# A decoder block with product-key experts: keys of four heads' choices looked up together, and a higher gather pace beside the choices

## The chip, the core and the metric

The kernel runs on one core of a Trainium2 chip. The core has TensorE (PE, matmul; PEld is its weight load), VectorE (DVE), ScalarE (ACT), GpSimd (POOL) and SyncE (SP), each with its own queue that it works off in order, and 16 DMA engines that all queues share. The metric is the device time of one execution in microseconds (us).

## The reference

One layer in float32, 512 tokens by 2048 features. Attention with a decay bias (8 heads) and a matrix-memory cell (4 heads) are projected, normalised and added; then comes the part that this change touches, a retrieval over 128 x 128 single-neuron experts:

```python
q = (xt @ w_q).reshape(T, PEER_HEADS, 2, PEER_KEY_DIM // 2)
scores = jnp.einsum('thpd,pnd->thpn', q, keys)
s_top, i_top = lax.top_k(scores, PEER_TOPK)          # 16 of 128, twice
cand = (s_top[:, :, 0, :, None] + s_top[:, :, 1, None, :])   # 16 x 16 sums
cand_idx = (i_top[:, :, 0, :, None] * PEER_N_KEYS + i_top[:, :, 1, None, :])
s_fin, pos = lax.top_k(cand, PEER_TOPK)              # 16 of the 256 sums
idx = jnp.take_along_axis(cand_idx, pos, axis=-1)    # which experts
gate = jax.nn.softmax(s_fin, axis=-1)
act = gelu(u[idx] . x) * gate;  y = sum(act * v[idx])
```

So for each of 512 tokens and 8 heads two lists of 16 keys are chosen, then 16 pairs out of their 256 sums. A pair's place `pos` is 16 * (place in the first list) + (place in the second); the lookup turns it into two key numbers, and 128 * first + second is the expert.

## The kernel before

The 512 tokens are four tiles of 128. After attention and cell (to about 620 us) comes the output projection, and with it the experts begin. They are worked in two ways at once.

- **Dense, on TensorE.** For token tiles 1 to 3 (less 64 tokens) all 16384 experts are multiplied: 128 blocks of 128 experts. `early_steps` loads a block in two chunks of 512 KB (`raw` or `rawx`, from `uT`); ScalarE rounds each to `hi` (L123), VectorE computes the rest `lo` (L125); 48 matmuls go into `sacc`; ScalarE applies gelu into `es` (L617) and stores 160 KB to `stab`. Later the gate of each chosen pair is spread over a table by one-hot matmuls (`table`, L963 to L973), and the same is done with `v`.
- **Gathered, on VectorE.** For tile 0 and the 64 tokens only the chosen rows are fetched: `gathered` issues one indirect DMA of 128 rows of 2048 floats (1 MB) on GpSimd's queue (L651), up to three rows ahead of their use, into `row` (three buffers) and, from the blocks on, every fourth into `rowx`; then `dot` multiplies it by x and sums (L662).

The two are interleaved by a step counter. `advance(n)` adds n to `state`, and each whole step issues the next gather and the dot product of an earlier row. A block calls it eight times with an eighth of `pace_u`. The paces are constants: 0.4 a hook in the output projection and in w_q, `PACE_EARLY` (1.25) a block beside the choices, 1.6 beside the tables; then what is left of 199 steps is divided over the blocks up to number 114 (26 of them), and the first 64 tokens' tables and `v` follow.

The choices of tiles 1 to 3 stand between. For each head `w_q(h)` multiplies out the queries and the scores of all three tiles; then, tile by tile, 2, 2 and 3 blocks of the dense part are issued (`EARLY_TOPK`) and `choose(t, h, scs)` follows: `top16` twice on 128 scores (five VectorE instructions each), the sum table `cd` on GpSimd (L751), `top16` on 256 sums, and the lookup. The lookup is done twice, for the first and the second list: shift or mask `pos` (L759), cast to float `pf` (L761), subtract 0 to 15 from each on GpSimd into `oh` (L763, 16 x 16), compare with zero and multiply by the list's keys `it` (L766), sum over the list (L769) into `i0f` or `i1f`. At the end `gates` makes a softmax of the scores of each tile, and TensorE transposes `i0f`, `i1f` and `gts` (L952) for the tables. Tile 0 is chosen earlier, between 780 and 960 us, by the same function, and its gathers wait for its heads.

Instructions are issued in the written order but placed on each engine's queue by a scheduler, which orders by readiness in its own model and moves `lo` ahead.

Of the kernel before, what the change touches and what calls it, by code (L numbers as in the profile page):

```python
# [10 lines left out]
F32 = mybir.dt.float32  # L11
# [3 lines left out]
U32 = mybir.dt.uint32  # L15
AF = mybir.ActivationFunctionType
OP = mybir.AluOpType
AX = mybir.AxisListType
PSUM = bass.MemoryType.PSUM

P = 128
S = 512
NT = S // P
# [8 lines left out]
TK = 16  # L32
PH = 8
# [13 lines left out]
EARLY_G = 3  # L47
HOLD = 14
PACE_O = 0.4
PACE_EARLY = 1.25  # L50
PACE_WQ = 0.4
PACE_G = 1.6
PACE_HOLD = 1.0
LAG = 2
LAG_U = 3
AHEAD_LO = 35
U_STEPS = SLOTS + S1 + 2 * LAG_U + 1
NTG = ND // TG

# [31 lines left out]
def block_kernel(ctx: ExitStack, tc: tile.TileContext, a, out):  # L91
    nc = tc.nc
# [7 lines left out]
    iota16 = iota[:, 0:TK]  # L100
# [485 lines left out]
    dots = [pc.tile([P, n], F32, name="dots%d" % t) for t, n in enumerate((SLOTS, S1))]  # L586
    act1 = pc.tile([P, P], F32, name="act1")
    tp = tpool(ctx, "tp")
    i0f = tp.tile([P, NT, PH, TK], F32, name="i0f")
    i1f = tp.tile([P, NT, PH, TK], F32, name="i1f")  # L590
    gts = tp.tile([P, NT, PH, TK], F32, name="gts")
    rows = tpool(ctx, "rows", 3)
    esp = tpool(ctx, "esp", 2)
# [117 lines left out]
    with ExitStack() as rx:  # L711
# [15 lines left out]
                add_block(xq.tile([P, 512], F32, tag="sq5", name="sq5"), acc[j], t, n)  # L727

        n2 = tpool(rx, "n2", 2)
        sc0 = n2.tile([P, PH, 2, P], F32, name="sc0", bufs=1)  # L730

        def top16(vals, idx, src, width):
            s2 = n2.tile([P, width], F32, tag="s2_%d" % width, name="s2")
# [4 lines left out]
            nc.vector.max_index(out=idx[:, 0:8], in_max=vals[:, 0:8], in_values=src)  # L738
            nc.vector.max_index(out=idx[:, 8:16], in_max=vals[:, 8:16], in_values=s2)

        def choose(t, h, scs):

            ii = n2.tile([P, 2, TK], U32, tag="ii", name="ii")
            vt = n2.tile([P, 2, TK], F32, tag="vt", name="vt")
            for j in range(2):
                top16(vt[:, j, :], ii[:, j, :], scs[:, j, :], P)
                yield
            it = n2.tile([P, 2, TK], F32, tag="it", name="it")
            nc.vector.tensor_copy(out=it, in_=ii)
            cd = n2.tile([P, TK, TK], F32, tag="cd", name="cd")  # L750
            nc.gpsimd.tensor_tensor(out=cd, in0=vt[:, 0, :, None].to_broadcast([P, TK, TK]),  # L751
                                    in1=vt[:, 1, None, :].to_broadcast([P, TK, TK]), op=OP.add)
            pos = n2.tile([P, TK], U32, tag="pos", name="pos")
            yield
            top16(gts[:, t, h, :], pos, cd.rearrange("p a b -> p (a b)"), TK * TK)
            yield
            for w, (op, imm) in enumerate(((OP.logical_shift_right, 4), (OP.bitwise_and, 15))):
                pi = n2.tile([P, TK], U32, tag="pi", name="pi")
                nc.vector.tensor_scalar(out=pi, in0=pos, scalar1=imm, scalar2=None, op0=op)  # L759
                pf = n2.tile([P, TK], F32, tag="pf", name="pf")  # L760
                nc.vector.tensor_copy(out=pf, in_=pi)  # L761
                oh = n2.tile([P, TK, TK], F32, tag="oh", name="oh")
                nc.gpsimd.tensor_tensor(out=oh, in0=pf[:, :, None].to_broadcast([P, TK, TK]),  # L763
                                        in1=iota16[:, None, :].to_broadcast([P, TK, TK]),
                                        op=OP.subtract)
                nc.vector.scalar_tensor_tensor(  # L766
                    out=oh, in0=oh, scalar=0.0, in1=it[:, w, None, :].to_broadcast([P, TK, TK]),
                    op0=OP.is_equal, op1=OP.mult)
                nc.vector.tensor_reduce(out=(i0f, i1f)[w][:, t, h, :], in_=oh, axis=AX.X,  # L769
                                        op=OP.add)  # L770
                if w == 1 and t == 0:
                    nc.vector.scalar_tensor_tensor(out=idx0[h], in0=i0f[:, 0, h], scalar=128.0,
                                                   in1=i1f[:, 0, h], op0=OP.mult, op1=OP.add)
                    heads0[0] = h + 1
                yield

        def gates(t):

            g = gts[:, t]
            top = n2.tile([P, PH], F32, tag="top", name="top")  # L780
            nc.vector.tensor_copy(out=top, in_=g[:, :, 0])
            nc.vector.tensor_tensor(out=g, in0=g, in1=top[:, :, None].to_broadcast([P, PH, TK]),
                                    op=OP.subtract)
            nc.scalar.activation(out=g, in_=g, func=AF.Exp)
            gs = n2.tile([P, PH], F32, tag="gs", name="gs")
            nc.vector.tensor_reduce(out=gs, in_=g, axis=AX.X, op=OP.add)
            nc.vector.reciprocal(out=gs, in_=gs)
            nc.vector.tensor_tensor(out=g, in0=g, in1=gs[:, :, None].to_broadcast([P, PH, TK]),
                                    op=OP.mult)
# [70 lines left out]
        def choose0_steps():  # L860
            for h in range(PH):
                while ready[0] <= h:
                    yield
                yield from choose(0, h, sc0[:, h])
            gates(0)

        scores0 = w_q0()
# [53 lines left out]
            next(chosen, None)  # L921
        for _ in chosen:
            pass
        for h in range(PH):
            scs = w_q(h)
            for t in range(1, NT):
                for _ in range(EARLY_TOPK[t - 1]):
                    early_s()
                for _ in choose(t, h, scs[t]):
                    pass  # L930
            if h == PH - 1:
                for t in range(1, NT):
                    gates(t)

        ix = n2.tile([P, SLOTS], I32, name="ix", bufs=1)
        nc.vector.scalar_tensor_tensor(out=ix, in0=flat(i0f[:, 1]), scalar=128.0,
# [255 lines left out]
```

## Time and profile before

| | |
|---|---|
| median of three runs | 3193.15 us (3188.04, 3193.15, 3195.32) |
| the profiled execution | 3191.11 us, its span 3189.3 us |
| granted TensorE clock | 0.992 of full, mean |
| busy: PE, DVE, ACT, POOL | 3108.9, 2324.3, 1274.7, 604.5 us |
| DMA | 835.71 MB, mean 262 GB/s |

The page is read from the totals to the stretches: a busy share over the whole span hides that the stages have different limits. The stages that matter here are the choices of tile 0 (780 to 960 us), those of tiles 1 to 3 with dense blocks (970 to 1500), the tables (1500 to 1790), 26 blocks with many gathers (1790 to 1990, called the full stretch below), and from about 2150 the products with `v`.

### The profile page before, as it was taken

Reading aid. Unit: us, or ns where it says so; the run is one execution under the profiler, and the core shown is the slowest. Engines: PE = TensorE matmul, PEld = TensorE weight load, DVE = VectorE, ACT = ScalarE, POOL = GpSimd, SP = SyncE. Lnnn points to the kernel's source line nnn. Section 1 sums busy time; section 2 is a strip of 40 time slices with the busy share of each in tenths; the row PEclk is TensorE's granted clock in tenths of the full one; section 3 lists DMA queues with packets and bytes.
Section 4 is the critical chain, followed back from the end, with each engine's and each line's share of the span. In section 5 each row is a group of like instructions: output and inputs, shape, how many; then the busy total and the mean of one; then the engine's idle time right before and its main releaser. Section 6 shows DMA issues by size and latency. Waiting matters only on the chain.

```text
span 3189.3 us, 43251 instructions
## 1 busy us (share of the span) xinstructions
PE 3108.9 (97%) x16682; PEld 2737.0 (86%) x16682; DVE 2324.3 (73%) x3251; ACT 1274.7 (40%) x1955; POOL 604.5 (19%) x444
## 2 busy tenths in 40 slices
PE   8999999999989999999999998989999999999998
PEld 6788777787779999999999988978888888888887
DVE  6533333456999999999898988757787777777764
ACT  4432222444443333334888632633333333333332
POOL 0000000100323333333222332112121122222200
PEclk9999999999999999999999999999999999999999
DMA  4222222256878888988999999899888888888753
GB/s 159 75 93 80 79 93 79 74 199 196 306 287 306 314 320 321 325 317 301 335 377 347 398 417 412 294 337 337 299 298 303 317 305 294 297 316 314 267 177 119
DMA packets 246577, 835.71 MB, mean 262 GB/s; under 512 B 21793, under 2 KB 104097, under 8 KB 200737
## 3 DMA queue, kind: packets, MB, share of 16 engines
q1 hardware_dynamic: 178402, 451.24, 41.9%
q0 software_dynamic: 46080, 335.56, 27.2%
q10 hardware_dynamic: 21888, 46.15, 3.8%
q8 instruction: 130, 2.13, 0.3%
q14 instruction: 77, 0.63, 0.1%
HBM read 781.94 MB, written 50.92 MB: 261 GB/s over the span
## 4 chain that ended last, share of the span: by engine, by line
PE 83%; DMA 7%; DVE 6%; issue 2%; ACT 2%; POOL 1%; SPq 0%; DVEq 0%; ACTq 0%; POOLq 0%
PE y L130 24%; PE acc L130 24%; PE sacc L130 20%; PE yk L130 8%; DMA row<-in_u,idx 4%; DVE lo L125 2%; DMA rowx<-in_u,idx 2%; DVE row L662 1%; PE sps L130 1%; PE po L130 1%; DMA sv<-stab 1%; ACT stg L971 1%; DMA gtB<-gtab 1%; ACT hi L123 1%; DMA raw<-in_uT 0%
## 5 line engine op out<-in xcount | busy, mean ns | idle before, releaser
L125 DVE TENSOR_TENSOR lo<-raw,hi 128x1024 fp32r<-128x1024 f32 x649 | 790.6, 1220 | 583.2 <-ACT hi L123 582.7
L123 ACT CAST hi<-raw 128x1024 fp32r<-128x1024 f32 x649 | 681.4, 1050 | 1295.9 <-PE y L130 388.3
L130 PE MATMUL sacc<-x3d,hi 128*128 128x320 f32 x4096 | 926.4, 313 | 4.6 <-ACT hi L123 4.6
L130 PEld LDWEIGHTS sacc<-x3d,hi 128*128 128x128 f32 x4096 | 687.0, 189 | 5.5 <-ACT hi L123 5.4
L130 PE MATMUL sacc<-x3d,lo 128*128 128x320 f32 x2048 | 643.1, 314 | 17.2 <-DVE lo L125 17.0
L130 PEld LDWEIGHTS sacc<-x3d,lo 128*128 128x128 f32 x2048 | 386.4, 189 | 28.9 <-DVE lo L125 28.2
L651 POOL DMA_INDIRECT row<-in_v,idx x128 | 217.4, 1699 | 839.2 <-ACT hi L123 605.2
L130 PE MATMUL y<-hi,wbufA 128*128 128x512 f32 x1152 | 357.7, 391 | 4.7 <-ACT hi L123 4.7
L662 DVE SCALAR_TENSOR_TENSOR row<-row,x 128x2048 f32<-128x2048 f32 x147 | 336.2, 2288 | 20.2 <-DMA row<-in_u,idx 20.1
L130 PE MATMUL y<-hi,wbufB 128*128 128x512 f32 x1128 | 349.1, 389 | 0.0
L692 DVE SCALAR_TENSOR_TENSOR x<-row,dots,x 128x2048 f32<-128x2048 f32 x128 | 300.1, 2344 | 0.0
L651 POOL DMA_INDIRECT row<-in_u,idx x147 | 194.8, 1325 | 500.0 <-ACT hi L123 222.2
L130 PEld LDWEIGHTS y<-hi,wbufA 128*128 128x128 f32 x1152 | 217.4, 189 | 50.5 <-ACT hi L123 5.1
L130 PEld LDWEIGHTS y<-hi,wbufB 128*128 128x128 f32 x1128 | 211.7, 188 | 44.0
L130 PE MATMUL acc<-xT,hi 128*128 128x512 f32 x768 | 244.1, 396 | 0.0
L130 PE MATMUL acc<-hi,xT 128*128 128x512 f32 x768 | 241.9, 393 | 0.0
L130 PE MATMUL y<-lo,wbufA 128*128 128x512 f32 x576 | 225.2, 391 | 1.9 <-DVE lo L125 1.9
L130 PE MATMUL y<-lo,wbufB 128*128 128x512 f32 x564 | 219.4, 389 | 0.0
L170 POOL TENSOR_TENSOR rsr<-rst,mhalf 128x1 f32<-128x1 f32 (+2 forms) x24 | 19.0, 796 | 893.4 <-DVE rst L167 893.4
L130 PEld LDWEIGHTS acc<-hi,xT 128*128 128x128 f32 x768 | 143.8, 188 | 28.7
L130 PEld LDWEIGHTS acc<-xT,hi 128*128 128x128 f32 x768 | 143.9, 189 | 28.4 <-ACT xT L187 0.2
L123 ACT CAST hi<-rawx 128x1024 fp32r<-128x1024 f32 x87 | 91.2, 1051 | 175.3 <-PE sacc L130 102.2
(550 smaller groups left out, 4592.4 us busy)
## 6 DMA issues: line engine op xcount, KB each, us to landing
raw<-in_vS SPq DMA_DIRECT2D x256, 512.0 KB
raw<-in_uT SPq DMA_DIRECT2D x177, 512.0 KB
rawx<-in_uT SPq DMA_DIRECT2D x79, 512.0 KB
raw<-in_w_out SPq DMA_DIRECT2D x64, 512.0 KB
raw<-in_w_q SPq DMA_DIRECT2D x56, 512.0 KB
gtab<-stg ACTq DMA_DIRECT2D x24, 1024.0 KB
stab<-es ACTq DMA_DIRECT2D x128, 160.0 KB
sv<-stab SPq DMA_DIRECT2D x64, 320.0 KB
```

The costliest lines, as they stand in the source:

```text
L123: pace[0] = nc.scalar.copy(out=hi[:, :width], in_=raw[:, :width]).ins
L125: nc.vector.tensor_tensor(out=lo[:, :width], in0=raw[:, :width], in1=hi[:, :width].bitcast(F32), op=OP.subtract)
L130: nc.tensor.matmul(out=o, lhsT=l, rhs=r, start=start, stop=stop)
L170: nc.gpsimd.tensor_tensor(out=r, in0=t, in1=mhalf[:, 0:width], op=OP.pow)
L651: beside(nc.gpsimd.indirect_dma_start(out=row, out_offset=None, in_=a[src], in_offset=bass.IndirectOffsetOnAxis(ap=idx(j), axis=0)))
L662: return nc.vector.scalar_tensor_tensor(out=row, in0=row, scalar=1.0, in1=x30, op0=OP.mult, op1=OP.mult, accum_out=to[:, j:j + 1])
L692: return nc.vector.scalar_tensor_tensor(out=x2[:, 0, :], in0=row, scalar=dots[0][:, j:j + 1], in1=x2[:, 0, :], op0=OP.mult, op1=OP.add)
L971: nc.scalar.copy(out=stg[:, :, q4 * 4:q4 * 4 + 4].rearrange("p i q -> p q i"), in_=gp_)
```

## The change

Three things change.

1. `choose` ends with the third `top16`; its positions go to a buffer (`posb`, four heads by three tiles). The keys of the lists are cast straight into their place in the results, one tile `i01` that holds `i0f` and `i1f`. For tiles 1 to 3 the lookup runs once for four heads: `decode_first` (shift or mask, cast, subtraction on GpSimd, now 128 x 1024) is issued after the fourth head's choice, for both lists; `decode_last` (compare, sum, written over the keys) one interval later, after the next tile's choice. The 128 x 1024 buffers of both lists are the space of `sc0`, the scores of tile 0. Tile 0 keeps a lookup for each head (`choose0`).
2. `pi` and `pf` have one buffer each, not two.
3. `PACE_EARLY` is 1.4, not 1.25. The step counter stands at 106 at the end of the choices where it stood at 98, and what is left for the 26 blocks of the full stretch is 1.73 steps a block where it was 2.04.

```diff
--- before.py
+++ after.py
@@ -47,13 +47,14 @@
 EARLY_G = 3
 HOLD = 14
 PACE_O = 0.4
-PACE_EARLY = 1.25
+PACE_EARLY = 1.4
 PACE_WQ = 0.4
 PACE_G = 1.6
 PACE_HOLD = 1.0
 LAG = 2
 LAG_U = 3
 AHEAD_LO = 35
+HB = PH // 2
 U_STEPS = SLOTS + S1 + 2 * LAG_U + 1
 NTG = ND // TG
 
@@ -586,8 +587,8 @@
     dots = [pc.tile([P, n], F32, name="dots%d" % t) for t, n in enumerate((SLOTS, S1))]
     act1 = pc.tile([P, P], F32, name="act1")
     tp = tpool(ctx, "tp")
-    i0f = tp.tile([P, NT, PH, TK], F32, name="i0f")
-    i1f = tp.tile([P, NT, PH, TK], F32, name="i1f")
+    i01 = tp.tile([P, 2, NT, PH, TK], F32, name="i01")
+    i0f, i1f = i01[:, 0], i01[:, 1]
     gts = tp.tile([P, NT, PH, TK], F32, name="gts")
     rows = tpool(ctx, "rows", 3)
     esp = tpool(ctx, "esp", 2)
@@ -727,7 +728,7 @@
                 add_block(xq.tile([P, 512], F32, tag="sq5", name="sq5"), acc[j], t, n)
 
         n2 = tpool(rx, "n2", 2)
-        sc0 = n2.tile([P, PH, 2, P], F32, name="sc0", bufs=1)
+        sc0 = n2.tile([P, PH, 2, P], F32, tag="sc0", name="sc0", bufs=1)
 
         def top16(vals, idx, src, width):
             s2 = n2.tile([P, width], F32, tag="s2_%d" % width, name="s2")
@@ -738,37 +739,55 @@
             nc.vector.max_index(out=idx[:, 0:8], in_max=vals[:, 0:8], in_values=src)
             nc.vector.max_index(out=idx[:, 8:16], in_max=vals[:, 8:16], in_values=s2)
 
-        def choose(t, h, scs):
+        def choose(t, h, scs, pos):
+
 
             ii = n2.tile([P, 2, TK], U32, tag="ii", name="ii")
             vt = n2.tile([P, 2, TK], F32, tag="vt", name="vt")
             for j in range(2):
                 top16(vt[:, j, :], ii[:, j, :], scs[:, j, :], P)
                 yield
-            it = n2.tile([P, 2, TK], F32, tag="it", name="it")
-            nc.vector.tensor_copy(out=it, in_=ii)
+            nc.vector.tensor_copy(out=i01[:, :, t, h, :], in_=ii)
             cd = n2.tile([P, TK, TK], F32, tag="cd", name="cd")
             nc.gpsimd.tensor_tensor(out=cd, in0=vt[:, 0, :, None].to_broadcast([P, TK, TK]),
                                     in1=vt[:, 1, None, :].to_broadcast([P, TK, TK]), op=OP.add)
-            pos = n2.tile([P, TK], U32, tag="pos", name="pos")
             yield
             top16(gts[:, t, h, :], pos, cd.rearrange("p a b -> p (a b)"), TK * TK)
             yield
-            for w, (op, imm) in enumerate(((OP.logical_shift_right, 4), (OP.bitwise_and, 15))):
-                pi = n2.tile([P, TK], U32, tag="pi", name="pi")
-                nc.vector.tensor_scalar(out=pi, in0=pos, scalar1=imm, scalar2=None, op0=op)
-                pf = n2.tile([P, TK], F32, tag="pf", name="pf")
-                nc.vector.tensor_copy(out=pf, in_=pi)
-                oh = n2.tile([P, TK, TK], F32, tag="oh", name="oh")
-                nc.gpsimd.tensor_tensor(out=oh, in0=pf[:, :, None].to_broadcast([P, TK, TK]),
-                                        in1=iota16[:, None, :].to_broadcast([P, TK, TK]),
-                                        op=OP.subtract)
-                nc.vector.scalar_tensor_tensor(
-                    out=oh, in0=oh, scalar=0.0, in1=it[:, w, None, :].to_broadcast([P, TK, TK]),
-                    op0=OP.is_equal, op1=OP.mult)
-                nc.vector.tensor_reduce(out=(i0f, i1f)[w][:, t, h, :], in_=oh, axis=AX.X,
-                                        op=OP.add)
-                if w == 1 and t == 0:
+
+        def decode_first(w, pos, oh):
+
+            n = pos.shape[1]
+            op, imm = ((OP.logical_shift_right, 4), (OP.bitwise_and, 15))[w]
+            pi = n2.tile([P, HB, TK], U32, tag="pi", name="pi", bufs=1)[:, 0:n]
+            nc.vector.tensor_scalar(out=pi, in0=pos, scalar1=imm, scalar2=None, op0=op)
+            pf = n2.tile([P, HB, TK], F32, tag="pf", name="pf", bufs=1)[:, 0:n]
+            nc.vector.tensor_copy(out=pf, in_=pi)
+            nc.gpsimd.tensor_tensor(
+                out=oh,
+                in0=pf.rearrange("p h k -> p k h")[:, :, :, None].to_broadcast([P, TK, n, TK]),
+                in1=iota16[:, None, None, :].to_broadcast([P, TK, n, TK]), op=OP.subtract)
+
+        def decode_last(w, t, hs, oh):
+
+            keys = i01[:, w, t, hs, :]
+            x = oh.rearrange("p k h i -> p k (h i)")
+            nc.vector.scalar_tensor_tensor(
+                out=x, in0=x, scalar=0.0,
+                in1=keys.rearrange("p h i -> p (h i)")[:, None, :].to_broadcast(list(x.shape)),
+                op0=OP.is_equal, op1=OP.mult)
+            nc.vector.tensor_reduce(out=keys.rearrange("p h k -> p k h"), in_=oh, axis=AX.X,
+                                    op=OP.add)
+
+        def choose0(h):
+
+            pos = n2.tile([P, 1, TK], U32, tag="pos", name="pos")
+            yield from choose(0, h, sc0[:, h], pos[:, 0])
+            for w in range(2):
+                oh = n2.tile([P, TK, 1, TK], F32, tag="oh", name="oh")
+                decode_first(w, pos, oh)
+                decode_last(w, 0, slice(h, h + 1), oh)
+                if w == 1:
                     nc.vector.scalar_tensor_tensor(out=idx0[h], in0=i0f[:, 0, h], scalar=128.0,
                                                    in1=i1f[:, 0, h], op0=OP.mult, op1=OP.add)
                     heads0[0] = h + 1
@@ -861,7 +880,7 @@
             for h in range(PH):
                 while ready[0] <= h:
                     yield
-                yield from choose(0, h, sc0[:, h])
+                yield from choose0(h)
             gates(0)
 
         scores0 = w_q0()
@@ -921,16 +940,36 @@
             next(chosen, None)
         for _ in chosen:
             pass
+        posb = n2.tile([P, NT - 1, HB, TK], U32, name="posb", bufs=1)
+        decoding = []
+
+        def decoded():
+            for t, hs, oh in decoding:
+                for w in range(2):
+                    decode_last(w, t, hs, oh[w])
+            decoding.clear()
+
         for h in range(PH):
             scs = w_q(h)
+            k = h % HB
             for t in range(1, NT):
                 for _ in range(EARLY_TOPK[t - 1]):
                     early_s()
-                for _ in choose(t, h, scs[t]):
+                for _ in choose(t, h, scs[t], posb[:, t - 1, k]):
                     pass
-            if h == PH - 1:
-                for t in range(1, NT):
-                    gates(t)
+
+                decoded()
+                if k == HB - 1:
+                    ohs = n2.tile([P, PH, 2, P], F32, tag="sc0", name="ohs", bufs=1)
+                    oh = [ohs.rearrange("p h j i -> p (h j i)")[:, w * HB * TK * TK:
+                                                               (w + 1) * HB * TK * TK]
+                          .rearrange("p (k h i) -> p k h i", k=TK, i=TK) for w in range(2)]
+                    for w in range(2):
+                        decode_first(w, posb[:, t - 1], oh[w])
+                    decoding.append((t, slice(h - k, h + 1), oh))
+        decoded()
+        for t in range(1, NT):
+            gates(t)
 
         ix = n2.tile([P, SLOTS], I32, name="ix", bufs=1)
         nc.vector.scalar_tensor_tensor(out=ix, in0=flat(i0f[:, 1]), scalar=128.0,
```

On GpSimd's queue in the middle of the choices (`row` and `rowx` are gathers; `cd` is the sum table of one choice, `oh` the subtraction of one lookup, `ohs` that of four heads), before and after:

```order
L651 DMA row<-in_u,idx_3_4834 128x2048
L763 TENSOR_TENSOR oh<-pf,cst 128x256 x2
L651 DMA row<-in_u,idx_3_4834 128x2048 x2
L651 DMA rowx<-in_u,idx_3_4834 128x2048
L751 TENSOR_TENSOR cd<-vt 128x256
L651 DMA row<-in_u,idx_3_4834 128x2048 x2
L763 TENSOR_TENSOR oh<-pf,cst 128x256 x2
L651 DMA row<-in_u,idx_3_4834 128x2048
L751 TENSOR_TENSOR cd<-vt 128x256
```

```order
L766 TENSOR_TENSOR ohs<-pf,cst 128x1024
L652 DMA row<-in_u,idx_3_4834 128x2048
L766 TENSOR_TENSOR ohs<-pf,cst 128x1024
L652 DMA row<-in_u,idx_3_4834 128x2048
L752 TENSOR_TENSOR cd<-vt 128x256
L652 DMA row<-in_u,idx_3_4834 128x2048
L766 TENSOR_TENSOR ohs<-pf,cst 128x1024
L652 DMA rowx<-in_u,idx_3_4834 128x2048
L766 TENSOR_TENSOR ohs<-pf,cst 128x1024
L652 DMA row<-in_u,idx_3_4834 128x2048 x2
```

Where two 128x256 subtractions stood after each sum table, three pairs of 128x1024 ones stand within some ten gathers, and for the next three heads none.

On VectorE's queue at the end of the choices (last choice, tile 3, head 7; `on` comes after). Before, the last rows; the last index search stands ten rows further up, shift and cast eight and six:

```order
L125 TENSOR_TENSOR lo<-raw,hi 128x1024
L787 RECIPROCAL gs<-gs 128x8
L786 TENSOR_REDUCE gs<-gts 128x8
L788 TENSOR_TENSOR gts<-gts,gs 128x128
L787 RECIPROCAL gs<-gs 128x8
L662 SCALAR_TENSOR_TENSOR rowx,dots_4841<-rowx,x_4830 128x2048
L766 SCALAR_TENSOR_TENSOR oh<-oh,it 128x256 x2
L769 TENSOR_REDUCE i0f<-oh 128x16
L769 TENSOR_REDUCE i1f<-oh 128x16
```

After, from the last index search on:

```order
L740 MAX_INDEX posb<-gts,s_13073 128x8
L800 COPY top<-gts 128x8 x2
L763 TENSOR_SCALAR pi<-posb 128x64
L801 TENSOR_TENSOR gts<-gts,top 128x128
L765 CAST pf<-pi 128x64
L801 TENSOR_TENSOR gts<-gts,top 128x128
L763 TENSOR_SCALAR pi<-posb 128x64
L126 TENSOR_TENSOR lo<-raw,hi 128x1024
L765 CAST pf<-pi 128x64
L775 SCALAR_TENSOR_TENSOR ohs<-ohs,i_4847 128x1024 x2
L779 TENSOR_REDUCE i_4847<-ohs 128x16x4 x2
L805 TENSOR_REDUCE gs<-gts 128x8 x2
```

The lookup stood behind other work, with a gather's dot product just ahead; now shift, cast, compare and sum of the last batch follow each other, with one `lo` between.

On TensorE's queue at the same place (`pt` are the transposes of keys and gates), the first transposes before, and those of tile 3's keys after:

```order
L130 MATMUL sacc<-x3d,lo 128x320
L952 MATMUL pt<-cst,i0f 128x128 x2
L952 MATMUL pt<-cst,i1f 128x128 x2
L952 MATMUL pt<-cst,gts 128x128
L130 MATMUL sacc<-x3d,hi 128x320 x2
L130 MATMUL sacc<-x3d,lo 128x320
L952 MATMUL pt<-cst,gts 128x128
```

```order
L131 MATMUL sacc<-x3d,hi 128x320 x2
L131 MATMUL sacc<-x3d,lo 128x320
L131 MATMUL sacc<-x3d,hi 128x320 x2
L991 MATMUL pt<-cst,i_4847 128x128 x2
L991 MATMUL pt<-cst,gts 128x128 x2
L131 MATMUL sacc<-x3d,lo 128x320
L131 MATMUL sacc<-x3d,hi 128x320 x2
```

Before, the keys of tiles 1 and 2 and then their gates come first, and tile 3's keys some 23 matmuls later. After, the gates stand behind tile 3's keys, which come some 25 matmuls after the others.

## Rows read from the trace of the kernel before

**Rows 1.** The page: its span and the busy time of each engine.
```profile
span 3189.3 us, 43251 instructions
...
PE 3108.9 (97%) x16682; PEld 2737.0 (86%) x16682; DVE 2324.3 (73%) x3251; ACT 1274.7 (40%) x1955; POOL 604.5 (19%) x444
```

**Rows 2.** Stretches: start:end, length, busy of each engine (count), TensorE clock, DMA share, GB/s.
```profile
780.00:960.00 180.00, 165.48 (x936) 143.90 (x935) 170.09 (x392) 88.20 (x121) 49.35 (x42) 0.98 0.83 291
970.00:1490.00 520.00, 520.00 (x3436) 518.35 (x3435) 490.60 (x1071) 180.61 (x235) 184.75 (x150) 1.00 0.90 320
1490.00:1500.00 10.00, 5.74 (x36) 5.27 (x36) 10.00 (x36) 4.53 (x7) 2.95 (x4) 0.94 0.91 328
1790.00:1990.00 200.00, 187.47 (x1206) 177.86 (x1205) 174.51 (x153) 65.38 (x86) 64.35 (x49) 0.99 1.02 418
```

**Rows 3.** Waits of VectorE (DVE), 1790 to 1990 us: us in total, times, longest.
```profile
DVE row L662 <- DMA row<-in_u,idx: 20.1, 30, 2.0
DVE rowx L662 <- DMA rowx<-in_u,idx: 5.3, 11, 1.7
```

**Rows 4.** Waits of TensorE (PE), 1790 to 1990 us.
```profile
PE sacc L130 <- DVE lo L125: 12.3, 20, 4.2
```

**Rows 5.** Timeline of ScalarE (ACT): two evictions beside the choices; start, us, what.
```profile
1472.78 0.43 ACT L617 ACTIVATE es<-sacc 128x320 f32<-128x320 f32 x1
...
1479.82 0.43 ACT L617 ACTIVATE es<-sacc 128x320 f32<-128x320 f32 x1
```

**Rows 6.** The full stretch, instructions on the tile sacc alone (PE, PEld, ACT).
```profile
1790.00:1990.00 200.00, 185.94 (x1190) 175.89 (x1189) 10.76 (x25) 0.99 1.02 418
```

**Rows 7.** DMA in the full stretch, 1800 to 1990 us.
```profile
DMA packets 17074, 79.37 MB, mean 418 GB/s; under 512 B 1899, under 2 KB 4885, under 8 KB 10836
```

**Rows 8.** Costliest groups, 970 to 1490 us: busy us, mean ns, idle before.
```profile
L662 DVE SCALAR_TENSOR_TENSOR row<-row,x 128x2048 f32<-128x2048 f32 x61 | 139.4, 2285 | 0.0
...
L125 DVE TENSOR_TENSOR lo<-raw,hi 128x1024 fp32r<-128x1024 f32 x92 | 111.5, 1212 | 19.2 <-ACT hi L123 19.2
...
L763 POOL TENSOR_TENSOR oh<-pf,cst 128x256 f32<-128x256 f32 x46 | 55.3, 1216 | 55.3 <-DVE pf L761 42.8 <-DVE pi L759 12.0
...
L766 DVE SCALAR_TENSOR_TENSOR oh<-oh,it 128x256 f32<-128x256 f32 x46 | 25.1, 576 | 8.9 <-POOL oh L763 8.8
```

**Rows 9.** Timeline of VectorE: one lookup (rows of other work left out).
```profile
1203.34 0.24 DVE L759 TENSOR_SCALAR pi<-pos 128x16 uint32<-128x16 uint32 x2
...
1205.70 0.24 DVE L761 CAST pf<-pi 128x16 f32<-128x16 uint32 x2
...
1207.59 1.16 DVE L766 SCALAR_TENSOR_TENSOR oh<-oh,it 128x256 f32<-128x256 f32 x2 [0.51 <-POOL oh L763]
1208.67 0.40 DVE L769 TENSOR_REDUCE i0f<-oh 128x16 f32<-128x256 f32 x1
1209.01 0.40 DVE L769 TENSOR_REDUCE i1f<-oh 128x16 f32<-128x256 f32 x1
```

**Rows 10.** The whole run's group of the 128x1024 TENSOR_TENSOR.
```profile
L963 DVE TENSOR_TENSOR on<-cst,idxT 128x1024 f32<-128x1024 f32 x96 | 116.7, 1221 | 29.6 <-PE gp__15871 L130 3.0 <-PE gp__19037 L130 1.8 <-PE gp__18706 L130 1.6
```

**Rows 11.** Waits of VectorE, 970 to 1490 us.
```profile
DVE lo L125 <- ACT hi L123: 19.2, 13, 2.9
```

**Rows 12.** Timeline of GpSimd (POOL): two subtractions of one lookup.
```profile
1224.52 1.52 POOL L763 TENSOR_TENSOR oh<-pf,cst 128x256 f32<-128x256 f32 x1 [4.40 <-DVE pf L761]
1226.67 0.62 POOL L763 TENSOR_TENSOR oh<-pf,cst 128x256 f32<-128x256 f32 x1 [0.62 <-DVE pf L761]
```

**Rows 13.** Timeline of VectorE: last index search and last key.
```profile
1494.07 0.41 DVE L739 FIND_INDEX8 pos<-gts,s 128x8 uint32<-128x256 f32 x1
...
1501.64 0.40 DVE L769 TENSOR_REDUCE i1f<-oh 128x16 f32<-128x256 f32 x1
```

**Rows 14.** Waits of TensorE, 1490 to 1500 us.
```profile
PE pt L952 <- DVE gts L788: 2.6, 1, 2.6
PE pt L952 <- DVE pf L761: 1.6, 1, 1.6
```

## The prediction

> **What bounds the kernel now.** I read the page's totals first [rows 1]: TensorE is busy for 3108.9 of 3189.3 us, so whatever this change does, it can only work on some 80 us in which TensorE stands, or runs late. No matmul is added or removed. So the next view is the table of stretches [rows 2], read for TensorE's column and beside it for the engine that is full where TensorE isn't. From 970 to 1490 us, where the choices of token tiles 1 to 3 run, TensorE is busy for all of 520 us although VectorE is at 490.6: the work that the change makes cheaper is hidden there. At its end, 1490 to 1500, TensorE has 5.74 of 10 us. From 1790 to 1990, long after the choices, TensorE has 187.5 of 200 us, and the DMA share is 1.02 at 418 GB/s, more than in any other row shown.
>
> That last stretch is what the pace change touches. In it VectorE waits 20.1 + 5.3 us for gathered rows that have not landed [rows 3], and TensorE waits for `lo` [rows 4]: VectorE works in order, so a `lo` that stands behind a dot product on a late row comes late. TensorE's waits (12.3 us) are smaller than the loss, because a matmul stream that is fed late is drawn as busy. I therefore size the loss by blocks: an undisturbed block of 48 expert matmuls takes 1479.82 - 1472.78 = 7.04 us [rows 5]; the stretch holds 25 evictions and 1190 matmuls [rows 6], 24.8 blocks, 174.6 us of work in 200. 25 us are lost.
>
> **The change part by part: the pace.** The step counter follows from the constants. Up to the end of the choices 12.8 steps come from the output projection (4 x 8 x 0.4), 12.8 from w_q (8 x 4 x 0.4), and 58 blocks give 72.5 at a pace of 1.25, 81.2 at 1.4: 98 steps before, 106 after. The tables add 30 x 1.6 = 48 in both. What is left of 199 is spread over 26 blocks: (199 - 146) / 26 = 2.04 a block before, (199 - 154) / 26 = 1.73 after. Eight gathers of 1 MB (128 rows of 2048 floats) leave the full stretch.
>
> A block there moves two uT chunks (1.05 MB), 0.16 MB of gelu scores and its gathers: 1.21 + 2.04 x 1.05 = 3.35 MB, at the 418 GB/s of [rows 7] 8.02 us. Measured: 200 / 24.8 = 8.06. Bytes alone explain the stretch. After: 1.21 + 1.73 x 1.05 = 3.03 MB, 7.24 us, hardly over TensorE's 7.04. So 26 x 0.8 = 20 us are on offer at most by bytes, 25 if no stall is left at all. Two nearly equal rates don't mesh without loss, and the last blocks still wait for the last dot products; I take 17 and keep 8 and 25 as ends.
>
> The eight gathers go into the 58 blocks beside the choices. A block there then moves 1.21 + 1.4 x 1.05 = 2.68 MB, 6.4 us at 418 GB/s against 7.04 of matmuls, so the DMA engines have room (share 0.90 at 320 GB/s now [rows 2]). On VectorE they cost 8 x 2.29 = 18 us [rows 8]. GpSimd has to issue eight more, some 10 us on an engine busy for 185 of 520.
>
> **The change part by part: the lookups.** They are what pays for that. One choice's lookup is now 0.24 + 0.24 + 1.16 + 0.40 + 0.40 = 2.44 us of VectorE [rows 9], some 2.05 where instructions overlap; 24 of them for tiles 1 to 3, 49 us. After there are six batches of two lookups. No 128x1024 form of these operations is in the trace, so I bound it: the compare from 1.22 us, the 128x1024 TENSOR_TENSOR [rows 10], to four times 576 ns [rows 8]; the reduction from 1.2 to 4 x 0.40. With 0.5 us for shift and cast a batch is 5.3 to 8.3 us, six are 32 to 50. VectorE saves 17 us at best and nothing at worst; I take 11. With the gathers it has 7 us more to do (1 to 19), out of 29 us in which it is idle now, 19.2 of them because it is ahead and waits for `hi` [rows 11]. TensorE should not notice: 0, with up to 8 if stalls cluster.
>
> GpSimd's subtraction is the other piece. It takes 0.62 us where VectorE leaves it alone and 1.52 where it doesn't [rows 12]; four times the elements is 1.2 to 5 us, twice in a row per batch. While the choices go on, the order puts a dot product, a `lo` or other choices between, and the result is wanted an interval later. Behind a batch on GpSimd's queue stand gathers, up to 5 us late; three rows are ahead of their use, some 15 us at 1.4 a block, so that is hidden.
>
> **The change part by part: the end of the choices.** The last batch has nothing to hide behind. Before, from the last index search (1494.07 + 0.41) to the last key (1501.64 + 0.40) VectorE takes 7.6 us, with a dot product and a `lo` between [rows 13]; TensorE doesn't wait for these keys, but for the gates of tiles 1 and 2 (2.6 + 1.6 us [rows 14]); by count, 36 matmuls [rows 2] where 68 fit, it loses 4.7. After, the order on VectorE has the second cast behind a `lo`, with the single `pf` buffer still to be read by GpSimd, and then both compares, both reductions and the gates in one row. Worked out: shift and cast 0.4, first subtraction with a `lo` in its way 3.5, cast, second subtraction against the first compare 3.5, compare 1.2, reductions 2.4: 11 us. TensorE comes to the key transposes of tile 3 after two tiles' transposes and some 25 matmuls (3.7 us), with no gates before them now, and would wait about 9. I put this at 5 us more than before, between -3 and +10.
>
> Token tile 0 keeps its lookups head by head, but with one `pf` buffer instead of two: the second cast waits for the first subtraction. From 780 to 960 us VectorE is busy for 170 of 180 and TensorE loses 14.5 [rows 2]; eight heads at some 0.5 us, part of it covered: +1 (-3 to +4).
>
> **The sum.** -17 + 0 + 5 + 1 = -11 us, on the profiled execution's 3191.1: 3180. The shown runs have a median of 3193.15, 2 us above it, so as a median I say 3181.
>
> **Rivals.**
> First, the pace change gives little: the stretch waits on the order, not on bytes. Each of 41 waits for a row costs 0.62 us [rows 3]; if that latency stays, eight gathers fewer save 8 x 0.62 = 5 us, the end of the choices takes them back, and the time is 3192. For it: the waits are spread evenly. Against it: 8.02 and 8.06 us a block. 0.20.
>
> Second, slower: the long subtractions make VectorE the bound beside the choices. Twelve of them, each with a cast or compare that must wait behind the single buffer for up to 4 us: 48 us, and 18 for the gathers less nothing saved, 66 against 29 us of idle VectorE. TensorE would lose 37, the end 5, and the stretch gives back 17: 3216. It decides where VectorE's added time exceeds 29 + 12 us. For it: the 46 subtractions take 1216 ns on average [rows 8], twice the 620 ns of one that VectorE leaves alone [rows 12]. Against it: the order has a dot product and two `lo`, 4.7 us [rows 8], between the casts. 0.10. The Trainium skill, "SBUF — State Buffer", Who interferes with whom, says that VectorE (with two SBUF inputs) and GpSimd take a shared port pair for a whole instruction, the other being blocked. By that, one 1024-wide subtraction holds VectorE four times as long, though a quarter as often; the rows on 1.52 and 0.62 us agree that GpSimd is held, and show no more.
>
> Third, the whole loss goes, and the choices end no later: -25, 3168. 0.10.
>
> Fourth, the DMA engines become the bound beside the choices. There they moved 320 GB/s at a share of 0.90 [rows 2], which would be 356 at a full share; 2.68 MB then take 7.5 us where a block's matmuls take 7.04, and 58 x 0.49 = 28 us are lost against 17 won: 3208. Against it: 418 GB/s held for 190 us in the full stretch [rows 7], where the load is of the same kinds. 0.02. The Trainium skill, "SBUF — State Buffer", Summary: rules for kernel authors, says the like, about 358 GB/s for transfers from HBM; by that a block would be 7.49 us. The trace's 418, on one core, differs, and the measurement decides.
>
> **How the numbers follow.** My forecast (3172 to 3190) has 0.58. A run of this kernel can tell about 0.2%, 6.4 us, from no change. The forecast's range is nearly all under 3186.8, with the third rival: faster 0.67. The first rival and the forecast's upper edge make no change 0.21; the second, the fourth make slower 0.12. The range is 3167 to 3197: it holds the third rival and the first, and leaves out the second and the fourth.
>
> **What would show it.** In the profile after: the stretch of 26 blocks some 15 to 20 us shorter, its DMA share at or below 1.0, VectorE's waits for gathered rows under 10 us, TensorE still full beside the choices with VectorE at 490 to 510 of 520 us, 1024-wide compares at 1.2 to 2.3 us, and TensorE standing some 9 us at the key transposes. The forecast is wrong if the stretch keeps 8 us a block, or if TensorE shows waits for `lo` between 970 and 1490.

## The result, and the profile after

The changed kernel is slower: 3208.93 us (median of 6 runs, 3207.33 to 3211.15) against 3191.74 us; the ratio is 1.0055, with a 95% interval of 1.0044 to 1.0066. The forecast was 3181, faster. The profiled execution took 3208.35 us.

The page after, its span and the busy time of each engine; [rows 1] are those of before:

```profile
span 3206.6 us, 43079 instructions
...
PE 3109.2 (97%) x16682; PEld 2740.2 (85%) x16682; DVE 2319.0 (72%) x3107; ACT 1274.3 (40%) x1955; POOL 601.1 (19%) x408
```

VectorE has 5 us less to do in all, TensorE the same. Stretches of after, with the columns of [rows 2]:

```profile
970.00:1490.00 520.00, 510.28 (x3334) 507.72 (x3333) 475.29 (x902) 174.84 (x229) 178.12 (x117) 0.99 0.88 324
1205.00:1210.00 5.00, 3.31 (x23) 3.05 (x21) 5.00 (x12) 1.82 (x3) 0.66 (x2) 1.00 0.95 329
1210.00:1215.00 5.00, 4.42 (x20) 4.43 (x21) 5.00 (x12) 0.00 (x0) 0.00 (x0) 0.66 0.44 144
1230.00:1235.00 5.00, 2.82 (x16) 2.82 (x17) 5.00 (x20) 0.89 (x2) 3.37 (x3) 1.00 0.57 175
1235.00:1240.00 5.00, 1.99 (x12) 1.67 (x10) 5.00 (x11) 1.05 (x1) 0.00 (x0) 1.00 0.92 382
1240.00:1245.00 5.00, 2.76 (x9) 2.77 (x10) 5.00 (x9) 0.00 (x0) 1.33 (x1) 0.62 0.33 110
1245.00:1250.00 5.00, 5.00 (x22) 5.00 (x21) 4.39 (x5) 1.05 (x1) 1.78 (x2) 0.70 0.62 208
1510.00:1540.00 30.00, 18.18 (x84) 16.17 (x85) 26.14 (x62) 5.02 (x8) 10.01 (x6) 0.72 0.42 148
1830.00:2030.00 200.00, 197.25 (x1336) 194.70 (x1335) 168.51 (x150) 75.03 (x105) 57.83 (x43) 1.00 1.01 406
```

The last row is the full stretch, and it does what was forecast: 197.25 of 200 us against 187.47. The loss lies beside the choices, in two places in which VectorE is full and TensorE isn't. In the mean of 970 to 1490 this does not show: VectorE is *less* busy there than before, 475.3 against 490.6.

Where the time went is read most exactly from the matmuls, of which both kernels have 16682: how much later than before the same one starts. The table has every kernel of this study, from its one profiled execution (that of e8 lies 7 us under the kernel's median and that of e2 5 us above, so these rows read low and high). After, e3, e4 and e6 issue the same instructions in the same order on every engine up to 1053 us, and yet stand at +2.5, +2.7, -0.7 and +3.9 at matmul 4500; so a single profiled execution places a figure to some 2 us either way.

```
matmul no.               4500   6000   6250   7750   8100   9750  11200  12200
before: starts at, us     972   1199   1239   1466   1523   1757   1991   2164
                       tile 0        4th hd        end   tables full str.  v
after                    +2.5   +2.5  +17.2  +17.1  +34.1  +39.3  +20.8  +18.2
e1 pace 1.4 alone        +0.2   +2.5   +2.4   +4.7   +6.6  +12.2   -7.0   -9.7
e2 lookups alone         +7.7   +8.2  +17.2  +18.1  +31.6  +37.7  +38.3  +38.6
e4 subtract on VectorE   -0.7   -0.7  +10.9  +10.9  +23.9  +29.0   +8.9   +6.6
e5 two pf buffers        -0.1   -0.1  +13.5  +13.6  +31.1  +36.3  +17.3  +16.6
e12 e4 and e5            -0.4   -0.4  +10.1  +10.1  +21.5  +26.7   +7.7   +4.0
e6 two heads together    +3.9   +4.7   +9.9  +14.7  +17.8  +20.2   -2.6   -6.1
e3 staggered             +2.7   +2.7   +3.3   +8.0  +12.1  +14.4   -9.1  -10.6
e7 e3 and e5             -1.4   -1.4   -0.8   +2.3   +5.9   +8.2  -15.1  -16.8
e9 e3, e4 and e5         -2.0   -2.0   -2.0   -0.1   +4.5   +6.9  -14.6  -18.0
e11 e9, short last batch -1.2   -0.4   -0.3   +3.6   +2.8   +5.7  -13.6  -17.7
e10 e9 at pace 1.55      +0.2   +1.2   +1.2   +4.2  +14.1  +14.4   -9.9  -13.0
e8 pace 1.55 alone       -2.2   +4.2   +6.9  +11.8  +14.1  +20.5   -3.8   -7.6
```

After loses 14.7 us between matmuls 6000 and 6250, where the fourth head is chosen, 17 at the end of the choices, 2.5 before matmul 4500, where tile 0 is chosen, and 5 in the tables. The full stretch gives back 18.5.

TensorE's waits in the fourth head (1204 to 1249 us; total, times, longest), then those at the end (1490 to 1540), answering to [rows 14]:

```profile
PE acc L131 <- DVE lo L126: 7.5, 2, 5.2
PE sacc L131 <- DVE lo L126: 2.3, 1, 2.3
```

```profile
PE pt L991 <- DVE i L779: 8.1, 4, 4.6
PE sacc L131 <- DVE lo L126: 5.7, 4, 1.9
PE pt L991 <- DVE gts L807: 0.4, 1, 0.4
```

In the fourth head these are 9.8 of 14.7 us. The rest is the clock: the values of 0.66, 0.62 and 0.70 above are means of stretches at 1.2 and at 2.4 GHz. At 1.2 GHz, half of full, are two stretches about the ends of two of the waits:

```profile
1210.45:1213.86 3.41, 3.29 (x12) 3.29 (x13) 3.41 (x9) 0.00 (x0) 0.00 (x0) 0.50 0.57 182
1241.17:1248.00 6.83, 5.76 (x18) 5.76 (x19) 6.83 (x7) 0.00 (x0) 2.91 (x1) 0.50 0.64 210
```

Half of TensorE's 3.29 + 5.76 us there is lost, an estimate of 4.5 us, so the waits of this place cost about half as much again as they show.

Why `lo` comes late stands in the timeline of VectorE in the same place (start, us, what; other rows left out):

```profile
1204.86 1.21 DVE L775 SCALAR_TENSOR_TENSOR ohs<-ohs,i 128x1024 f32<-128x1024 f32 x1
...
1206.71 1.20 DVE L779 TENSOR_REDUCE i<-ohs 128x64 f32<-128x1024 f32 x1
...
1217.98 0.18 DVE L765 CAST pf<-pi 128x64 f32<-128x64 uint32 x1
1218.09 1.22 DVE L126 TENSOR_TENSOR lo<-rawx,hi 128x1024 fp32r<-128x1024 f32 x1
1219.22 2.05 DVE L763 TENSOR_SCALAR pi<-posb 128x64 uint32<-128x64 uint32 x1
1221.20 2.28 DVE L663 SCALAR_TENSOR_TENSOR rowx<-rowx,x 128x2048 f32<-128x2048 f32 x1
...
1223.41 0.18 DVE L765 CAST pf<-pi 128x64 f32<-128x64 uint32 x1
...
1226.86 4.12 DVE L663 SCALAR_TENSOR_TENSOR row<-row,x 128x2048 f32<-128x2048 f32 x1
...
1230.91 1.21 DVE L126 TENSOR_TENSOR lo<-raw,hi 128x1024 fp32r<-128x1024 f32 x1
...
1234.39 1.35 DVE L775 SCALAR_TENSOR_TENSOR ohs<-ohs,i 128x1024 f32<-128x1024 f32 x1
...
1235.75 1.21 DVE L775 SCALAR_TENSOR_TENSOR ohs<-ohs,i 128x1024 f32<-128x1024 f32 x1
...
1237.22 1.20 DVE L779 TENSOR_REDUCE i<-ohs 128x64 f32<-128x1024 f32 x1
...
1239.45 1.20 DVE L779 TENSOR_REDUCE i<-ohs 128x64 f32<-128x1024 f32 x1
...
1240.97 1.21 DVE L126 TENSOR_TENSOR lo<-raw,hi 128x1024 fp32r<-128x1024 f32 x1
```

Between the `lo` of 1230.91 and that of 1240.97 lie 10 us in which VectorE searches for tile 3 and looks up tile 2. VectorE has no idle time in these rows. The batches of all three tiles stand in this one head. GpSimd beside it:

```profile
1218.92 2.30 POOL L766 TENSOR_TENSOR ohs<-pf,cst 128x1024 f32<-128x1024 f32 x1
...
1225.57 3.26 POOL L766 TENSOR_TENSOR ohs<-pf,cst 128x1024 f32<-128x1024 f32 x1
```

The shift that began at 1219.22 ended at 1221.27, with the subtraction (1218.92 + 2.30), and took 2.05 us, where the same kernel's undisturbed shifts take 0.19; the dot product of 1226.86 took 4.12 where 2.28 is usual, and ended 2.15 us after the subtraction (1228.83). Six instructions of 1195 to 1256 us are longer by 1.8 to 1.9 us each beside a subtraction, 11 us in all.

The full stretch, 1830 to 2030 us: waits of VectorE for rows and of TensorE for `lo`, answering to [rows 3] and [rows 4] (25.4 and 12.3 there), then the instructions on sacc, to [rows 6]:

```profile
DVE row L663 <- DMA row<-in_u,idx: 11.8, 18, 1.7
DVE rowx L663 <- DMA rowx<-in_u,idx: 1.9, 4, 0.5
```

```profile
PE sacc L131 <- DVE lo L126: 2.3, 5, 1.3
```

```profile
1830.00:2030.00 200.00, 194.74 (x1306) 191.54 (x1306) 11.59 (x27) 1.00 1.01 406
```

1306 matmuls are 27.2 blocks in 200 us, 7.35 us each in place of 8.06; forecast were 7.24 by bytes.

### The profile page after: what moved, and what is told of

The parts are those of the page before. It is cut to its first block, busy times and chain, and to the rows that moved or that the text cites. A ratio compares the mean times of both kernels' runs of the same rounds, so it can differ in the third digit from the quotient of the medians.

```text
span 3206.6 us, 43079 instructions
## 1 busy us (share of the span) xinstructions
PE 3109.2 (97%) x16682; PEld 2740.2 (85%) x16682; DVE 2319.0 (72%) x3107; ACT 1274.3 (40%) x1955; POOL 601.1 (19%) x408
## 4 chain that ended last, share of the span: by engine, by line
PE 44%; DMA 4%; ACT 2%; DVE 1%; issue 1%; SPq 0%; ACTq 0%; DVEq 0%; POOLq 0%; POOL 0%
PE y L131 24%; PE sacc L131 10%; PE yk L131 8%; DMA raw<-in_uT 2%; DMA row<-in_u,idx 1%; ACT stg L1010 1%; ACT og L1007 1%; DVE lo L126 0%; ACT hi L124 0%; DMA gtB<-gtab 0%; DMA raw<-in_vS 0%; DMA sv<-stab 0%; DVE row L663 0%; DVE x L693 0%; SPq L118 0%
## 5 line engine op out<-in xcount | busy, mean ns | idle before, releaser
L131 PE MATMUL sacc<-x3d,lo 128*128 128x320 f32 x2048 | 643.5, 314 | 15.4 <-DVE lo L126 14.9
L652 POOL DMA_INDIRECT row<-in_u,idx x147 | 211.6, 1440 | 546.1 <-ACT hi L124 246.1
```

The costliest lines, as they stand in the source:

```text
L131: nc.tensor.matmul(out=o, lhsT=l, rhs=r, start=start, stop=stop)
L652: beside(nc.gpsimd.indirect_dma_start(out=row, out_offset=None, in_=a[src], in_offset=bass.IndirectOffsetOnAxis(ap=idx(j), axis=0)))
```

## The experiments

Four theories, each with its rivals. A1: three tiles' lookups in one head are a burst longer than VectorE can make up for. A2: GpSimd's long subtractions hold VectorE. B: the additional dot products do it. C: the single `pf` buffer. All ratios are to the kernel before, whose medians in the groups of runs are 3190.0 to 3191.7 us, so that medians of different groups can be set against each other to within 2 us.

**The two parts by themselves.** e1 is the kernel before with one number changed, e2 the changed kernel with it changed back:

```
-PACE_EARLY = 1.25      -PACE_EARLY = 1.4
+PACE_EARLY = 1.4       +PACE_EARLY = 1.25
```

> The kernel before with the pace of the gathers beside the choices at 1.4 in place of 1.25; the lookups stay per head. Theory A (the lookups of three tiles fall into one head, and VectorE is late with the split products there; the pace itself is sound): the gain of the full stretch is kept and nothing is lost beside the choices, 3170 to 3176 us. Theory B (the additional dot products are what VectorE cannot carry where the matmuls stand still): the loss beside the choices comes with the pace, 3190 to 3205 us.

3180.80 us, 0.9969 (0.9958 to 0.9981): faster, but between the two theories' figures.

> The changed kernel with the pace at 1.25, so only the lookups of four heads together are left of the change. Theory A: both losses of about 15 us beside the choices stay and the gain of the full stretch goes, 3215 to 3230 us. Theory B: the losses need the additional gathers, 3188 to 3198 us.

3224.59 us, 1.0107 (1.0090 to 1.0123), as theory A said. The lookups make the loss, and B is out as its only cause: in the table e2 has the two steps without the additional gathers, at 9.0 and 13.5 us. With the gathers they are 14.7 and 17, so by these executions the dot products enlarge them. The pace makes the full stretch (9750 to 11200) 19.2 us shorter in e1 and leaves it in e2 (+0.6). But e1 also loses 12 us before it, 5.6 of them in the tables. Its VectorE beside the choices, 970 to 1490 us, the stretch and one wait, where [rows 2] and [rows 11] have 490.60 and 19.2:

```profile
970.00:1490.00 520.00, 517.11 (x3404) 513.58 (x3403) 506.48 (x1077) 178.07 (x232) 211.16 (x157) 1.00 0.92 333
```

```profile
DVE lo L125 <- ACT hi L123: 3.3, 5, 0.7
```

VectorE's waits for `hi`, the sign that it is ahead, have gone from 19.2 to 3.3 us: it is nearly the bound there.

**The burst taken apart.** e3 ends the batches of the three tiles in different heads, for which the batch has n heads in place of HB:

```
+STARTS = ((0, 2, 6), (0, 3, 7), (0, 4))
...
-                if k == HB - 1:
+                if last:      # h + 1 in STARTS[t - 1], or the last head
+                    n = k + 1
```

> The changed kernel, but the lookups of the three tiles end in different heads: tile 1 after heads 2, 6 and 8, tile 2 after 3, 7 and 8, tile 3 after 4 and 8 (one more batch for each of tiles 1 and 2). Theory A1 (what hurts is that three lookups fall into one head): the loss of 15 us in the middle goes, the one at the end shrinks, 3182 to 3196 us. Theory A2 (each long subtraction of GpSimd holds VectorE up for about 2 us, wherever it stands, and VectorE has no room for that): no better, 3204 to 3214 us.

3179.28 us, 0.9964 (0.9951 to 0.9976): A1, and better than its range. The step in the fourth head is 0.6 us in place of 14.7, that at the end 4.1 in place of 17; 4.7 are lost between them. The same number of heads is looked up, and GpSimd's subtractions take 37.0 us in sum, in after 35.6. e6 has HB = 2:

> The changed kernel with the lookups of two heads together (four batches of three tiles, instructions of 128x512) in place of four. Theory A1 (a burst longer than what the split buffers bridge): each burst is half as long, its loss far less than half, so about 0 to 3 us in each of the first three places and 5 to 8 at the end, 3186 to 3197 us. Theory A2 (each held VectorE instruction costs time, in proportion to GpSimd's time, which stays the same in sum): 3203 to 3211 us.

3183.02 us, 0.9974 (0.9964 to 0.9984): A1 again, below its range. Half the burst loses 5.2 us in the fourth head, a third of 14.7, and 3.1 at the end in place of 17; another 4.8 go between them.

**GpSimd's hold.** In e4 the twelve long subtractions are VectorE's:

```
-            nc.gpsimd.tensor_tensor(
+            (nc.vector if n > 1 else nc.gpsimd).tensor_tensor(
```

> The changed kernel with the twelve subtractions of 128x1024 on VectorE in place of GpSimd. Theory A2 (lengthening by the long GpSimd subtractions): some 11 us of lengthened VectorE instructions go in the middle and 5 at the end, and 6 subtractions of about 1.2 us come in each place, 3198 to 3206 us. Theory A1 (amount of VectorE work within one head): 7 us of VectorE work are added in each of the two heads, 3212 to 3224 us.

3198.07 us, 1.0026 (1.0015 to 1.0036): the edge of A2's range. So A2 holds as well, as a second cause: VectorE has more instructions, and the kernel is 11 us faster than the changed one. Not all of that is the hold. Of the 11.6 us in the table 3.2 come before matmul 4500, where the edit has changed nothing; the two steps shrink by 3.1 and 4.0 us. In these lookups the edit also takes GpSimd's reads from the single `pf` buffer; with two buffers in both kernels (e5 and e12, below) it is worth 7.0 us. The groups of VectorE in e4 (970 to 1540 us; busy us, mean ns), then those of after:

```profile
L775 DVE SCALAR_TENSOR_TENSOR ohs<-ohs,i 128x1024 f32<-128x1024 f32 x12 | 15.1, 1254 | 0.0
L766 DVE TENSOR_TENSOR ohs<-pf,cst 128x1024 f32<-128x1024 f32 x12 | 14.6, 1217 | 0.0
L779 DVE TENSOR_REDUCE i<-ohs 128x64 f32<-128x1024 f32 x12 | 14.4, 1202 | 0.0
L763 DVE TENSOR_SCALAR pi<-posb 128x64 uint32<-128x64 uint32 x12 | 2.2, 186 | 0.0
```

```profile
L766 POOL TENSOR_TENSOR ohs<-pf,cst 128x1024 f32<-128x1024 f32 x12 | 35.6, 2966 | 17.8 <-DVE pf L765 17.7
L775 DVE SCALAR_TENSOR_TENSOR ohs<-ohs,i 128x1024 f32<-128x1024 f32 x12 | 17.9, 1495 | 1.9 <-POOL ohs L766 1.9
L779 DVE TENSOR_REDUCE i<-ohs 128x64 f32<-128x1024 f32 x12 | 14.3, 1202 | 0.0
L763 DVE TENSOR_SCALAR pi<-posb 128x64 uint32<-128x64 uint32 x12 | 7.9, 656 | 0.0
L765 DVE CAST pf<-pi 128x64 f32<-128x64 uint32 x12 | 2.2, 187 | 1.9 <-POOL ohs L766 1.9
```

Twelve subtractions cost VectorE 14.6 us. Left to GpSimd they lengthen VectorE's instructions beside them by 17.8 us in after (worked out from the trace, each against the lower quartile of its kind); of these the rows above show 2.8 in the compares and 5.7 in the shifts.

**The single buffer.** In e5 `pf` takes turns in the two buffers of another tile:

```
-            pf = n2.tile([P, HB, TK], F32, tag="pf", name="pf", bufs=1)[:, 0:n]
+            pf = n2.tile([P, TK * TK], F32, tag="s2_256", name="pf")[:, 0:n * TK]
```

> The changed kernel, but the positions as floats (pf), which GpSimd's subtraction reads, take turns in two buffers for every tile; in the changed kernel they have one, and the second cast waits for the first subtraction. Theory C (the one buffer pulls the pairs of tile 0 apart and makes the 4.5 us lost at the end of tile 0's choices): that loss goes, 3202 to 3206 us, and in the batches the 1.9 us waits of pf go too while the lengthened instructions stay. Rival (the loss at tile 0 is chance of order): 3207 to 3211 us.

3204.30 us, 1.0043 (1.0028 to 1.0057): in theory C's range and 4.6 us under after, though the intervals overlap. The step at tile 0 goes (+2.5 becomes -0.1); in the burst little is won (13.6 in place of 14.7). The casts no longer wait 1.9 us, but take 5.9 us in place of 2.2, so they are held instead (970 to 1540 us, e5):

```profile
L766 DVE CAST pf<-pi 128x64 f32<-128x64 uint32 x12 | 5.9, 490 | 0.0
```

That the buffer makes the loss at tile 0 is likely and not settled: e4 has one buffer there and stands at -0.7. e7 has the second buffer with e3:

> The staggered kernel with two buffers for pf. If the 4.4 us that it loses at the end of tile 0 come from the one buffer: 3173 to 3177 us, faster than the pace alone (3181). If not: 3178 to 3181 us.

3176.04 us, 0.9958 (0.9941 to 0.9974), 3 us under e3, as expected, though the intervals overlap.

**Sums.** e9 is e7 with e4's edit (a batch of one head, of which it has one, keeps its subtractions on GpSimd), e12 is e5 with it:

> The staggered kernel with two buffers for pf and the long subtractions on VectorE. With the bursts apart, VectorE has idle time in each head: if GpSimd's hold on VectorE costs no time there, the added 14 to 18 us of VectorE work cost nothing either or a little, 3173 to 3180 us; if the hold still costs time, this is 3 to 6 us faster than the same kernel with the subtractions on GpSimd.

3172.37 us, 0.9944 (0.9928 to 0.9961): 3.7 us under e7, though the intervals overlap. Its place of the fourth head, 1195 to 1255 us, is whole again (after has 50.28 of 60 us there):

```profile
1195.00:1255.00 60.00, 60.00 (x395) 59.79 (x395) 59.72 (x116) 20.61 (x27) 14.28 (x14) 1.00 0.88 333
```

> The changed kernel with two buffers for pf and the long subtractions on VectorE, the three tiles' lookups still in the same heads. If the causes found so far add up (hold of GpSimd 11 us, buffer 4.6 us, both taken from 3209): 3192 to 3195 us, and what is left against the staggered kernel with the same two edits (3172) is the burst alone, about 20 us. If the burst was mostly GpSimd's hold: 3180 to 3188 us.

3197.29 us, 1.0022 (1.0012 to 1.0031): neither case's range. The two edits do not add up: with the subtraction on VectorE the second buffer gives nothing measurable, and the subtraction gives 7.0 us beside it (against e5). Against e9, in which the same lookups stand in different heads (in eight batches instead of six), 25 us remain: that is what the burst costs without GpSimd's hold, the largest cause. Of the 22 us that the table shows of it, 15.4 are lost between matmuls 4500 and 8100, beside the choices; the rest lies before them, in the tables and in the full stretch, and is not explained.

**How far it goes.**

> The kernel before with the pace at 1.55. If the full stretch pays for each gather that is taken out of it and VectorE beside the choices loses about half of that again (1.4 gave 10 of 20 us): 3174 to 3181 us. If beside the choices VectorE is at its end at 1.4: 3182 to 3200 us.

3189.76 us, 0.9994 (0.9984 to 1.0004): no gain left, the second case. Beside the choices VectorE is busy for 510 of 520 us and hardly waits for `hi`:

```profile
970.00:1490.00 520.00, 510.08 (x3338) 504.26 (x3337) 510.22 (x1071) 173.92 (x226) 211.77 (x161) 1.00 0.93 341
```

```profile
DVE lo L125 <- ACT hi L123: 0.2, 1, 0.2
```

> The staggered kernel with two buffers and the subtractions on VectorE, pace 1.55. The lookups of more heads together leave VectorE idle time beside the choices; if this idle time carries further dot products: 3155 to 3168 us. If the next heads' bursts are in the way: 3170 to 3180 us.

3176.74 us, 0.9953 (0.9936 to 0.9970): the second case, no better than at 1.4. The full stretch has 24.3 us less than before, near the 25 that the prediction put as its end; the end of the choices loses 10.

> The staggered kernel with two buffers and the subtractions on VectorE, but only one head of each tile is left for the last lookups, and the gates stand ahead of them. If the last four heads' lookups of tile 3 make the 5 us lost at the end of the choices: 3165 to 3169 us. If these 5 us are of the choices themselves and the gates: 3171 to 3175 us.

3173.47 us, 0.9944 (0.9928 to 0.9961): no gain over e9. The time is in the second case's range, but the loss at the end did go with the lookups, as the first case has it: by the table the end is 5 us better, and what lies ahead of it 4 us worse. The kernel has twelve batches in place of eight, and the five of one head keep their subtractions on GpSimd. e9 and e11 are the fastest kernels here, 0.56% under the one before.

## Why the prediction was wrong

**The full stretch: right.** -17 was said, -18.5 measured (9750 to 11200), with 7.35 us a block against 7.24 and row waits of 13.7 us (under 10 was said). e2 shows that it is the pace's.

**Beside the choices: the step that failed**, in the words of the prediction: "TensorE should not notice: 0, with up to 8 if stalls cluster". Its amounts were within their ends: the twelve shifts, casts, compares and reductions of after are 7.9 + 2.2 + 17.9 + 14.3 = 42.3 us, of 32 to 50, and over the whole run VectorE is busy for 2319.0 us against 2325.9 in e1, which has the same pace: 6.9 saved, where 11 was taken of 0 to 17. The error was to set this sum against 29 us of idle time spread over 520. All batches of the three tiles end in the fourth and the eighth head. One head has 29.4 / 8 = 3.7 us of idle time [rows 2], and 1.7 at the new pace (13.5 / 8, e1); three batches of 2 x (0.19 + 0.19 + 1.25 + 1.20) = 5.7 us, less three lookups of 2.05, add 11, and GpSimd's hold 11 more. 22 us met at most 3.7. Since 14.7 were lost, some 7 us are bridged, by that idle time and by the split products already made; in e4 18 us of added work lost 11.6. The six other heads became lighter. Against the kernel before that was worth nothing, as TensorE was full there already; against e1, which loses 2.3 us in each of 4500 to 6000 and 6250 to 7750, it saved these 4.6.

**The second rival had the sign and the time** (3216), and half of the mechanism: the held VectorE is shown by e4 and e12, worth 7 to 11 us, but it is not the whole; its price, 48 us of waits at the single buffer, is not what the trace has (1.9 us before the casts and 1.9 before the compares), so it is in part luck that 3216 came near. The case against it, that a dot product and two `lo` stand between the casts, was true of the order (a `lo`, the shift and a dot product in the timeline) and no protection: these themselves were held. The row in [rows 12] was read for what it did to GpSimd alone. The Trainium skill, "SBUF — State Buffer", Who interferes with whom, says that whoever takes the shared port pair first has it for its whole instruction, and that the issue order decides who blocks; the trace agrees, with a shift of 2.05 us ending with GpSimd's subtraction. The same section of the Trainium skill has reductions on trn2 never contending, and the twelve at 1202 ns in both after and e4 agree.

**The end of the choices**: 5 was said, 17 measured (7750 to 8100). The wait for keys has the size that was said (9, measured 8.1) by luck: it was to be tile 3's alone, and the trace has 5.6 us at tile 2's keys and 2.5 at tile 3's. What was left out is that the batches of tiles 1 and 2 stand just ahead of it, so `lo` is late as well (5.7 us), and that the clock then stays low (0.72 in 1510 to 1540). e3 has seven heads' lookups there in place of twelve, and loses 4.1.

**Tile 0**: +1 (-3 to +4) said. The four kernels that are the same up to there, with one buffer, stand at -0.7 to +3.9 at matmul 4500, those with two buffers at -2.0 to +0.2: some 3 us by the means, if the buffer makes them.

**The first rival** (order, not bytes) is out by the 18.5 us, and so is the fourth (DMA): beside the choices the share is 0.88, and 0.92 in e1. The third (-25) came near only in e10, with 24.3 in the full stretch.

Open: after loses 5 us in the tables (8100 to 9750), as do e1 and e2 (5.6 and 6.1), while e3, e7 and e9 lose 2.3 to 2.4. TensorE stands there for 5.9 us in after, nearly all of it for `og`, under 1.3 us each, against 3.0 in the kernel before and 4.3 in e9; that is about half of the loss. No run was made on it.

## What to carry to other kernels

Compare added work with idle time in the interval in which it falls, not over the whole stretch: work that is bunched costs its peak, and the troughs that it leaves elsewhere give back only what was short there. Where several streams have the same period, shift their phases; here the same lookups, with the subtraction on VectorE, cost 16 us against the pace alone when they stood together (e12 against e1), and staggered they were 8 us faster than it (e9, with intervals that just touch). And before work goes to GpSimd to relieve VectorE, compare its price on VectorE with what VectorE's other instructions lose beside it.

## What the runs showed of the hardware

GpSimd's subtraction against its size, beside a busy VectorE: 1216 ns at 256 elements a partition [rows 8], 2092 at 512 (24 of them in e6), 2966 at 1024; together 57, 50 and 36 us for the same elements. On VectorE the 1024 take 1217 ns. GpSimd's time falls with larger pieces, and what VectorE loses rises: its instructions beside these subtractions are longer by 11.3 us in sum in the kernel before, 15.7 in e6 and 17.8 in after (each against the lower quartile of its kind).

TensorE's wait of 2.3 us (to 1210.58) and that of 5.2 us (to 1242.24) end within stretches at 1.2 GHz of 3.4 and 6.8 us, which lost some 1.6 and 2.9 us by the clock; beside the wait of 2.2 us (to 1232.18) the clock stayed at 2.4 GHz.
